# A column roll on one core: long row pieces spread over 13 DMA engines instead of 16

## The chip, the core and the metric

The kernel runs on one core of one Trainium2 chip. The metric is device time in microseconds (us) of one execution, and lower is better. A core has 16 DMA engines, which the profile counts together; SP and ACT issue transfers on one hardware queue each (q1 and q10 in the profile), and POOL (GpSimd) issues on a software queue (q0). TensorE does nothing in this kernel.

## What is computed

```python
x = np.random.randn(8192, 8192).astype(np.float32)   # 268.4 MB
shift = 100
return np.roll(x, shift, axis=1)
```

Every row of 8192 numbers (32 KB) is moved 100 places to the right, and its last 100 numbers come to its front. Nothing is calculated; 268.4 MB are read from HBM and 268.4 MB are written.

## The kernel before, in words

The kernel cuts each output row in two. With `s = 100`, the cut is at `a = 256` (line 20 rounds 100 up to 128, line 22 adds 128), and `g = a - s = 156`.

**Long pieces** are columns 256 to 8191 of the output: 7936 numbers, 31,744 bytes for each row. They go from HBM to HBM without a stop in SBUF. The rows are cut into 128 blocks of 64. A block is viewed as `e=16` groups of `j=4` neighbouring rows, and one `dma_start` on line 43 takes row `j` of all 16 groups: 16 rows of 31,744 bytes, whose starts are 4 rows apart. Rows with even `j` are issued by SP and rows with odd `j` by ACT. In the last four blocks each piece is cut into two halves of 15,872 bytes at `mid`. Per queue that makes 248 transfers of full pieces and 16 of halves. The framework lets each queue have four of its transfers under way: the issue of one waits until the fourth before it has landed (the first wait of each queue stands behind four issues).

**Heads** are columns 0 to 255 of the output, 8.4 MB in all. They go through SBUF, in 16 steps `k` of 512 rows. Per step POOL issues three reads: `t` (line 72), for three of every four rows one contiguous run of 256 numbers that holds the end of the row before and the start of the row itself; and two short reads into `h` (lines 73 and 76) for the rest. DVE copies both parts of `t` to their places in `h` (lines 74 and 77). All `t` and `h` tiles have buffers of their own, so nothing waits for a buffer. After the last read POOL issues 16 writes of `h` to the output (line 80), each as 512 rows of 1 KB. All head transfers have 128 partitions, or 512 rows, as their outer dimension.

Nothing else orders the three queues among each other. There is no other work.

Of the kernel before, what the change touches and what calls it, by code (L numbers as in the profile page):

```python
# [1 line left out]

# [4 lines left out]


@with_exitstack
def kernel(  # L10
    ctx: ExitStack,
    tc: tile.TileContext,
    x: bass.AP,
    shift: int,
    out: bass.AP,
):
    nc = tc.nc
    n_rows, n_cols = x.shape
    s = shift % n_cols
    a = -(-s // 128) * 128  # L20
    if 0 < a <= 384 and a + 128 <= n_cols:
        a += 128
    g = a - s
    P = nc.NUM_PARTITIONS
    engines = [nc.sync, nc.scalar]
    n_chunks = 16
    rows = n_rows // n_chunks

    xm = x.rearrange("(c e j) w -> c j e w", e=16, j=4)
    om = out.rearrange("(c e j) w -> c j e w", e=16, j=4)
    if a < n_cols:
        blocks = n_rows // 64
        mid = (a + n_cols) // 256 * 128
        for c in range(blocks):
            parts = ((a, mid), (mid, n_cols)) if c >= blocks - 4 and a < mid else ((a, n_cols),)  # L40
            for j in range(4):
                for lo, hi in parts:
                    engines[j % 2].dma_start(out=om[c, j, :, lo:hi], in_=xm[c, j, :, lo - s:hi - s])
    if a == 0:
        return


    if a > 512:
        for i in range(n_chunks):
            r = slice(i * rows, (i + 1) * rows)  # L50
            nc.gpsimd.dma_start(out=out[r, :s], in_=x[r, n_cols - s:])
            if g > 0:
                nc.gpsimd.dma_start(out=out[r, s:a], in_=x[r, :g])
        return

    Q = 4  # L60
    n_st = n_rows // (P * Q)
    reads = ctx.enter_context(tc.tile_pool(name="reads", bufs=n_st))
    heads = ctx.enter_context(tc.tile_pool(name="heads", bufs=n_st))
    xt = x.rearrange("(k p q) c -> k p q c", q=Q, p=P)
    ot = out.rearrange("(k p q) c -> k p q c", q=Q, p=P)
    tiles = []
    for k in range(n_st):
        t = reads.tile([P, Q - 1, a], x.dtype)
        h = heads.tile([P, Q, a], x.dtype)
        lead = bass.AP(tensor=x.tensor, offset=(k * P * Q + 1) * n_cols - s,  # L70
                       ap=[[Q * n_cols, P], [n_cols, Q - 1], [1, a]])
        nc.gpsimd.dma_start(out=t[:], in_=lead)  # L72
        nc.gpsimd.dma_start(out=h[:, Q - 1, :s], in_=xt[k, :, Q - 1, n_cols - s:])  # L73
        nc.vector.tensor_copy(h[:, :Q - 1, :s], t[:, :, :s])  # L74
        if g > 0:
            nc.gpsimd.dma_start(out=h[:, 0, s:], in_=xt[k, :, 0, :g])  # L76
            nc.vector.tensor_copy(h[:, 1:, s:], t[:, :, s:])  # L77
        tiles.append(h)
    for k, h in enumerate(tiles):
        nc.gpsimd.dma_start(out=ot[k, :, :, :a], in_=h[:])  # L80


# [1 line left out]
_INS = ['x', 'shift']  # L84
_OUTS = [((8192, 8192), 'float32')]

_NUMBERS = {'shift': 100}


# [26 lines left out]
```

## Time and profile before

| what | value |
|---|---|
| time, median of 3 runs | 816.8 us (815.75 to 818.27) |
| span of the profiled execution, first to last instruction | 828.0 us |
| DVE busy / POOL busy | 12.3 us / 41.3 us |
| bytes moved by DMA | 276.90 MB, mean 334 GB/s |
| HBM read + written | 268.44 MB + 268.44 MB, 648 GB/s over the span |

The median is of runs that were not profiled. For the profiled execution the page gives the span alone: its transfers begin 2.1 us after the span's start and the last of them ends 1.3 us before the span's end, so the span is taken as its own time. It is 11.2 us (1.4%) above the median.

A transfer from HBM to HBM counts once in the GB/s of the DMA lines, and twice (read and written) in HBM traffic. A "packet" of the long pieces is one row: 31,744 bytes carried by one DMA engine. After each there is a packet of 4 bytes that counts the transfer's completion, so half of the packets of q1 and q10 are these. The share in the queue lines is the time of the packets as a share of 16 engines' time.

### The profile page before, as it was taken

Reading aid. Unit: us, or ns where it says so; the run is one execution under the profiler, and the core shown is the slowest. Engines: PE = TensorE matmul, PEld = TensorE weight load, DVE = VectorE, ACT = ScalarE, POOL = GpSimd, SP = SyncE. Lnnn points to the kernel's source line nnn. Section 1 sums busy time; section 2 is a strip of 40 time slices with the busy share of each in tenths; the row PEclk is TensorE's granted clock in tenths of the full one; section 3 lists DMA queues with packets and bytes.
Section 4 is the critical chain, followed back from the end, with each engine's and each line's share of the span. In section 5 each row is a group of like instructions: output and inputs, shape, how many; then the busy total and the mean of one; then the engine's idle time right before and its main releaser. Section 6 shows DMA issues by size and latency. Waiting matters only on the chain. (4 is left out here: it accounts for less than half of the span.)

```text
span 828.0 us, 689 instructions
## 1 busy us (share of the span) xinstructions
DVE 12.3 (1%) x32; POOL 41.3 (5%) x68
## 2 busy tenths in 40 slices
DVE  0000000000010000000000000000000000000000
POOL 2011000000021100000000000000000000000000
DMA  9999999999999999999999999999999999999998
GB/s 308 340 350 334 344 340 337 337 339 344 337 342 348 352 351 345 354 339 346 347 341 344 333 325 325 319 330 333 330 324 322 335 330 328 322 331 328 327 314 300
DMA packets 22278, 276.90 MB, mean 334 GB/s; under 512 B 9473, under 2 KB 9729, under 8 KB 13825
## 3 DMA queue, kind: packets, MB, share of 16 engines
q1 hardware_dynamic: 8448, 130.04, 46.1%
q10 hardware_dynamic: 8448, 130.04, 44.7%
q0 software_dynamic: 5376, 16.78, 8.4%
q14 instruction: 6, 0.04, 0.0%
HBM read 268.44 MB, written 268.44 MB: 648 GB/s over the span
## 5 line engine op out<-in xcount | busy, mean ns | idle before, releaser
L80 POOL DMA_DIRECT2D out_dram<-h x16 | 11.5, 724 | 126.6 <-DMA out_dram<-h 86.8
L76 POOL DMA_DIRECT2D h<-in_x_dram x16 | 8.7, 542 | 141.4 <-DMA t<-in_x_dram 141.4
L72 POOL DMA_DIRECT2D t<-in_x_dram x16 | 12.2, 762 | 30.8 <-DMA h<-in_x_dram 30.0
L73 POOL DMA_DIRECT2D h<-in_x_dram x16 | 8.9, 559 | 39.9 <-DMA h<-in_x_dram 39.9
L74 DVE COPY h<-t 128x300 f32<-128x300 f32 x16 | 6.1, 382 | 260.2 <-DMA t<-in_x_dram 260.2
L77 DVE COPY h<-t 128x468 f32<-128x468 f32 x16 | 7.5, 467 | 0.0
L97 POOL MEMSET const-float32-0.0<- 128x1 f32 x1 | 0.1, 99 | 0.2 <-issue 0.2
L97 POOL MEMSET const-bfloat16-1.0<- 128x1 bf16 x1 | 0.1, 102 | 0.0
L97 POOL MEMSET const-float32-1.0<- 128x1 f32 x1 | 0.1, 99 | 0.0
L97 POOL MEMSET const-uint8-127<- 128x1 uint8 x1 | 0.1, 99 | 0.0
## 6 DMA issues: line engine op xcount, KB each, us to landing
out_dram<-in_x_dram ACTq DMA_DIRECT2D x248, 496.0 KB, 12.7
out_dram<-in_x_dram SPq DMA_DIRECT2D x248, 496.0 KB, 12.7
out_dram<-h POOLq DMA_DIRECT2D x16, 512.0 KB, 108.2
t<-in_x_dram POOLq DMA_DIRECT2D x16, 384.0 KB, 50.6
out_dram<-in_x_dram SPq DMA_DIRECT2D x16, 248.0 KB, 6.0
out_dram<-in_x_dram ACTq DMA_DIRECT2D x16, 248.0 KB, 5.9
h<-in_x_dram POOLq DMA_DIRECT2D x16, 78.0 KB, 43.2
h<-in_x_dram POOLq DMA_DIRECT2D x16, 50.0 KB, 49.9
```

The lines of the kernel that those rows point to most:

```text
L72: nc.gpsimd.dma_start(out=t[:], in_=lead)
L73: nc.gpsimd.dma_start(out=h[:, Q - 1, :s], in_=xt[k, :, Q - 1, n_cols - s:])
L74: nc.vector.tensor_copy(h[:, :Q - 1, :s], t[:, :, :s])
L76: nc.gpsimd.dma_start(out=h[:, 0, s:], in_=xt[k, :, 0, :g])
L77: nc.vector.tensor_copy(h[:, 1:, s:], t[:, :, s:])
L80: nc.gpsimd.dma_start(out=ot[k, :, :, :a], in_=h[:])
L97: nc = _bacc.Bacc("TRN2", target_bir_lowering=False, num_devices=1)
```

## The change

The long pieces of the first rows are issued in blocks of 52 rows, viewed as `e=13` groups of `j=4` rows. One transfer then has 13 rows of 31,744 bytes instead of 16. `K * 4` is 52; the rest of 8192 rows after whole blocks of 52 is 28, and the loop adds 52 until the tail is a multiple of 16 and at least 256, which is 288. So the code takes 152 blocks of 52 rows, 7904 rows in all, and then 288 rows as before with `e=16`: one block of 64 with whole pieces, and the last 224 rows in halves. (A short description that came with the change speaks of 7696 and 496 rows; the code gives 7904 and 288.) Per queue that is 304 transfers of 13 whole rows, 2 of 16 whole rows and 14 of 16 halves. The heads, with POOL's and DVE's instructions and their order, are the same.

```diff
+    K = 13
+    tail = n_rows % (K * 4)
+    while tail % 16 or tail < 256:
+        tail += K * 4
 
+    def copies(r0, e, js, halves):
+        xm = x[r0:r0 + e * js, :].rearrange("(e j) w -> j e w", j=js)
+        om = out[r0:r0 + e * js, :].rearrange("(e j) w -> j e w", j=js)
+        mid = (a + n_cols) // 256 * 128
+        parts = ((a, mid), (mid, n_cols)) if halves and a < mid else ((a, n_cols),)
+        for j in range(js):
+            for lo, hi in parts:
+                if lo < hi:
+                    engines[j % 2].dma_start(out=om[j, :, lo:hi], in_=xm[j, :, lo - s:hi - s])
 
-    xm = x.rearrange("(c e j) w -> c j e w", e=16, j=4)
-    om = out.rearrange("(c e j) w -> c j e w", e=16, j=4)
-    if a < n_cols:
-        blocks = n_rows // 64
-        mid = (a + n_cols) // 256 * 128
-        for c in range(blocks):
-            parts = ((a, mid), (mid, n_cols)) if c >= blocks - 4 and a < mid else ((a, n_cols),)
-            for j in range(4):
-                for lo, hi in parts:
-                    engines[j % 2].dma_start(out=om[c, j, :, lo:hi], in_=xm[c, j, :, lo - s:hi - s])
+    r0 = 0
+    while r0 + tail < n_rows:
+        copies(r0, K, 4, False)
+        r0 += K * 4
+    while r0 < n_rows:
+        js = min(4, (n_rows - r0) // 16)
+        copies(r0, 16, js, r0 + 256 >= n_rows)
+        r0 += 16 * js
```

## The prediction

> **What bounds the kernel now.** I read the page first, then the queue lines of single stretches of the span, then the waits of the issuing queue.
>
> ```profile
> span 828.0 us, 689 instructions
> DMA  9999999999999999999999999999999999999998
> ...
> q1 hardware_dynamic: 8448, 130.04, 46.1%
> q10 hardware_dynamic: 8448, 130.04, 44.7%
> q0 software_dynamic: 5376, 16.78, 8.4%
> ...
> HBM read 268.44 MB, written 268.44 MB: 648 GB/s over the span
> ```
>
> All 16 DMA engines are busy from end to end: 46.1 + 44.7 + 8.4 = 99.2%. No compute engine matters (DVE 12.3 us). But "busy" has two meanings here: an engine that moves at its own pace, or one whose packet is stretched by something shared. Three stretches tell them apart: heads being read, heads being written, long pieces alone.
>
> ```profile
> q10 hardware_dynamic: 2277, 36.03, 41.8%
> q1 hardware_dynamic: 2303, 36.35, 40.3%
> q0 software_dynamic: 2738, 7.55, 17.6%
> ```
>
> This is 5 to 240 us. Long pieces hold 82.1% of 16 engines, 13.1 engines' worth. Their packets took 0.821 x 16 x 235 = 3087 us, and 72.38 MB / 31,744 B = 2280 of them make 1.354 us each. HBM traffic is (2 x 72.38 + 7.55) / 235 us = 648 GB/s.
>
> ```profile
> q1 hardware_dynamic: 2325, 37.11, 46.3%
> q10 hardware_dynamic: 2309, 36.61, 42.8%
> q0 software_dynamic: 2611, 9.14, 11.7%
> ```
>
> 240 to 480 us: 14.3 engines' worth, by the same working 1.473 us a packet, 652 GB/s.
>
> ```profile
> q1 hardware_dynamic: 2892, 45.94, 50.8%
> q10 hardware_dynamic: 2893, 45.88, 48.5%
> ```
>
> 500 to 780 us, no heads: 15.9 engines' worth, 1.538 us a packet, 656 GB/s. From start to start it is 280 x 16 / 2892 = 1.549 us, so 0.011 us is lost between packets.
>
> ```profile
> q10 hardware_dynamic: 16, 0.51, 102.2%
> ```
>
> 3.5 to 4.7 us, the second packet of each engine: 1.022 x 16 x 1.2 / 16 = 1.226 us. The shortest long packet among the trace's records is 1.17 us (27.1 GB/s for one engine).
>
> So a packet that needs 1.17 to 1.23 us takes 1.35 with 13 engines on long pieces and 1.54 with 16, while the traffic stays at 648 to 656 GB/s. That is a shared limit near 656: more engines make each slower. Three engines fewer may therefore cost little. But the margin is small, and the sum below goes by one engine's load.
>
> ```profile
> SPq L43 <- DMA out_dram<-in_x_dram: 680.3, 260, 4.9
> ...
> L43 SPq DMA_DIRECT2D out_dram<-in_x_dram x264: 509/510/832, 0.7 to 820.3; - x132
> ```
>
> SP mostly waits for transfers to land (680.3 of 828 us), and an issue costs it 0.51 us.
>
> **The change part by part.**
>
> *Issuing.* Per queue 264 issues become 320 (304 + 2 + 14): 56 x 0.51 = 29 us more on SP and on ACT. The 680 us of waiting hide it; a transfer is issued every 828 / 320 = 2.6 us. Without that cover it would be 29 us. The window of four transfers a queue holds 13/16 of the bytes, but still 8 packets for each engine in use, so no engine on long pieces runs dry sooner. POOL and DVE do what they did, cost 0.
>
> *Load of one engine.* Before: 8192 / 16 = 512 rows and one sixteenth of the heads. After, an engine that is used: 7904 / 13 = 608 rows, 288 / 16 = 18 rows of the tail, and the same heads. The three others have heads and tail only, and are idle most of the time. Faster heads on these three end nothing sooner, since a head transfer lands when its last part does. So the end is set by the 13.
>
> *Heads.* 8.4% of 828 = 69.6 us an engine today. The reading stretch cost 0.176 x 16 x 235 = 662 us for 7.55 MB, the writing one 0.117 x 16 x 240 = 449 us for 9.14 MB; if reads became as cheap as writes, 16.78 MB x 49 us / 16 = 51 us. I take 70 for no relief, 51 for the range.
>
> *A long packet while heads are under way.* The 13 engines spend about a sixth of this stage on heads, so some 11 are on long pieces at a time, less than the 13.1 of the first stretch. Bounds: 1.17 (shortest) and 1.354 (that stretch). I take 1.23, the row of the second packets, and 1.24 with the gap.
>
> *A long packet with no heads.* Below, the ceiling: 13 x 31,744 B x 2 / 656 GB/s = 1.258 us. Above, 1.354 of the first stretch, where as many engines were on long pieces and head traffic came on top. The uncrowded pace would ask for 13 x 27.1 x 2 = 705 GB/s, more than any long stretch carried, so some crowding must stay. The first stretch, with all 16 engines at work, reached 648; fewer requesters should not come closer to the ceiling. I take the middle, 1.306, and 1.316 with the gap.
>
> *Sum.* The last head write was issued at 379.6 us and took some 108 us, so heads end near 488; packets ahead of theirs shrink by about a tenth, so 440. In that stage (440 - 70) / 1.24 = 298 long packets. The other 310 take 310 x 1.316 = 408 us. Tail 18 x 1.55 = 28 us, start and end 3.4 us (as now). 440 + 408 + 28 + 3.4 = 879 us of span. The median stood at 816.8 / 828.05 = 0.9864 of the span: 867 us. Ends of this case: 1.18 with heads and the ceiling's 1.268 after give 844.6, so 833 us; 1.364 in both stages gives 931, so 918 us.
>
> The Trainium skill speaks on both sides. "DMA: Bandwidth & Descriptors", Rules for kernel authors, tells an author to use all 16 engines and to choose the outer dimension for that, which speaks against 13; taken alone, as if engines were the limit, it makes the long rows 608/512 as dear. The same page's Specifications put one engine at about 27 GiB/s, 29 GB/s; by that a packet could take 1.10 us, an estimate, and 13 engines would carry 377 GB/s, more than the 328 of the last stretch, so nothing would be lost. The trace's best packet, 27.1 GB/s, is below that figure, and its crowded ones are at 20.6, so neither is used in the sum.
>
> **The rivals.**
>
> *Crowding goes with the three engines (faster).* All packets fall to 1.17 us and 0.011 of gap: 608 x 1.181 + 70 + 31.4 = 819 span, 808 us; with heads at 51, 800 and 789 us. It decides below a slot of (828 - 31.4 - 70) / 608 = 1.195 us, or 1.226 with the cheap heads. For it: the second packets at 1.226 and the many records at 1.17 even in the last stretch. Against: it needs some 670 GB/s on average where no stretch passed 656. A limit that falls with the number of streams could do this; 648, 652 and 656 at 13.1, 14.3 and 15.9 engines' worth don't show one.
>
> *Packets don't get shorter (much slower).* If the 1.538 us belongs to each engine and its neighbours, not to a total: 608 x 1.549 + 70 + 31.4 = 1043, 1029 us. Against: the 1.354 of the first stretch.
>
> *The 13 rows don't stay on 13 engines.* If successive transfers start on other engines, all 16 share the rows as before. Then the rate is that of now, about 817 us. No row of this trace names an engine. The Trainium skill ("DMA: Bandwidth & Descriptors", on why a DMA increments its semaphore by 16) says that hardware queues use the lowest-numbered k engines, k being the largest divisor up to 16, here 13; no run so far shows it.
>
> **How the numbers follow.** A difference of 0.3%, 2.5 us, is about what the runs can tell from none. The forecast has 0.76 (833 to 918, all slower), the much slower case 0.06, rotation 0.06 (no change), the gain 0.12. The range leaves out the slowest case, the last few us of the forecast, and about half of the gain: 808 to 914, with 867 as the likeliest. Faster 0.12, same 0.06, slower 0.82.
>
> **What the profile after would show.** Right: DMA share near 13.3 of 16 engines (tenths of 8 and 9), about 315 GB/s in the stretches without heads, some 1.3 us from start to start over 13 engines, and full sharing only in the last 30 us; heads done before 488 us. The forecast is wrong if the share stays at 99% (rotation), if the last stretches carry over 335 GB/s (crowding gone), or if they carry under 290 (packets not shorter). Of the steps, the packet with no heads is the weakest: 0.05 us on it moves the end by 15 us.

## The result and the profile after

| | median | runs |
|---|---|---|
| before | 817.95 us | 6 (815.75 to 819.06) |
| changed | 823.01 us | 6 (820.65 to 826.37) |

The changed kernel takes 1.0067 times as long, 95% interval 1.005 to 1.0083: slower, as forecast, but by 5 us and not by 50.

Page of the changed kernel (the DMA row in tenths of 16 engines, then the queues with packets, MB and share):

```profile
span 821.5 us, 801 instructions
DMA  7888888888888888888888788888888888888898
...
q1 hardware_dynamic: 8416, 130.04, 39.3%
q10 hardware_dynamic: 8416, 130.04, 38.0%
q0 software_dynamic: 5376, 16.78, 6.1%
...
HBM read 268.44 MB, written 268.44 MB: 653 GB/s over the span
```

The engines are now busy for 83% instead of 99% (39.3 + 38.0 + 6.1 = 83.4%, 13.3 of 16 engines, as the prediction had it), and the bytes arrive in almost the same time. That fits rows that stay on 13 engines, since 13/16 is 81%; run 4 settles it. Heads hold 6.1% where they held 8.4%.

Queue lines of the changed kernel, 5 to 240 us, then 500 to 780 us:

```profile
q1 hardware_dynamic: 2271, 36.26, 37.0%
q10 hardware_dynamic: 2273, 35.91, 36.0%
q0 software_dynamic: 3267, 9.14, 12.8%
```

```profile
q1 hardware_dynamic: 2909, 46.19, 41.4%
q10 hardware_dynamic: 2916, 46.38, 40.1%
```

With the prediction's working: while heads are read a long packet takes 0.730 x 16 x 235 / 2273 = 1.21 us (1.354 before), and without heads 0.815 x 16 x 280 / 2916 = 1.25 us (1.538 before). Without heads the HBM traffic is 2 x 92.57 MB / 280 us = 661 GB/s; as one-way bytes that is 331 GB/s, between the 315 that the prediction expected and the 335 above which it called itself wrong.

Waits of SP's queue, and its issues (duration in ns, minimum, median, maximum):

```profile
SPq L43 <- DMA out_dram<-in_x_dram: 567.1, 316, 3.8
...
L43 SPq DMA_DIRECT2D out_dram<-in_x_dram x320: 509/764/982, 0.7 to 814.1; - x160
```

An issue of 13 rows costs 0.76 us where one of 16 rows cost 0.51. With 56 more issues SP spends some 110 us more on issuing (320 x 0.764 against 264 x 0.51, an estimate from the medians), not 29, and its waits shrink by as much, from 680.3 to 567.1 us. It still waits for 567 us, so this is covered.

### The profile page after: what moved, and what is told of

Same layout as the page of the kernel before. It is cut to its first block, busy times and chain, and to the rows that moved or that the text cites. A ratio compares the mean times of both kernels' runs of the same rounds, so it can differ in the third digit from the quotient of the medians.

```text
span 821.5 us, 801 instructions
## 1 busy us (share of the span) xinstructions
DVE 12.0 (1%) x32; POOL 41.2 (5%) x68
## 3 DMA queue, kind: packets, MB, share of 16 engines
q1 hardware_dynamic: 8416, 130.04, 39.3%
q0 software_dynamic: 5376, 16.78, 6.1%
```

## The experiments

Times below are compared only within one set of runs on one chip. The kernel before itself took 826.4, 826.7 and 816.4 us in the three sets, and 818.0 beside the result.

**1. The kernel before, profiled again** (no edit).

> The kernel before, profiled once more, because its first profiled execution (span 828.0 us) stands 1.2% above its own median while the changed kernel's profiled span (821.5 us) is close to its median of 823.0. Expected: a span of about 816 us, long packets without heads at 1.52 us instead of 1.538, HBM traffic there of about 661 GB/s, as with 13 engines. If the span is 828 again, profiling itself costs this kernel 1.4% and the changed kernel nothing.

Median 826.67 us, its profiled span 824.0, and without heads 1.53 us a packet and 658 GB/s. The level of this set is 1% above that of the result; the expectation of 816 us missed. The profiled execution was one of the timed ones: 825.8 us of time for 824.0 of span, so what lies around the span is some 2 us. Profiling has no cost of 1.4%. So the 828.0 us and the 816.8 us from which the prediction took its ratio of 0.9864 are probably of two levels of speed; the time of that first profiled execution is not on record.

**2 to 4. Other numbers of engines.** In each, `K = 13` becomes `K = 14` (below), `12` or `8`, and the tail follows by its own rule.

```diff
-    K = 13
+    K = 14
```

> K = 14 instead of 13: 7840 rows on 14 engines, 352 on 16. Theory S (one shared limit of about 661 GB/s of HBM traffic, packets stretch until they fit into it, an engine alone needs 1.18 us): packets without heads 14 x 63.5 KB / 661 GB/s = 1.345 us, same traffic, time between those of 16 and 13 engines, 816 to 823 us. Rival F (fewer streams use HBM better, so 13 gains in the stretches and loses elsewhere): traffic without heads below that of 13 engines, by 1% or more.

> K = 12: 7920 rows on 12 engines, 272 on 16. Theory S: 12 engines at their own pace ask for 12 x 63.5 KB / 1.19 us = 640 GB/s, below the limit, so the engines are the bound all through: packets 1.18 us, 660 x 1.19 + 26 + 50 + 3 = 865 us of span, 5% slower than 13. Rival F: crowding stays even below the limit, packets stay at 1.22 us or more, 890 us or more.

> K = 8: 7936 rows on 8 engines, 256 on 16. It measures a packet that nothing crowds. Theory S: nearly every packet at 1.174 to 1.18 us, 992 x 1.19 + 25 + 45 + 3 = 1253 us, traffic without heads 8 x 63.5 / 1.19 = 427 GB/s. Rival F, or neighbours on the same engines' ports that hinder each other: a mean above 1.2 us, over 1270 us. If the rows did not stay on 8 engines, the time would be near 820 us.

| engines | time | ratio to before (95%) | long packet without heads | HBM traffic there |
|---|---|---|---|---|
| 16 (run 1) | 826.67 us | 1.0004 (0.9989 to 1.0019) | 1.53 us | 658 GB/s |
| 14 | 831.71 us | 1.006 (1.004 to 1.0079) | 1.35 us | 658 GB/s |
| 12 | 862.89 us | 1.044 (1.0419 to 1.0461) | 1.20 us | 637 GB/s |
| 8 | 1252.21 us | 1.5152 (1.5109 to 1.5196) | 1.20 us | 427 GB/s |

The last two columns come from the queue lines of 500 to 780 us. Those with 16 engines, 14, 12 and 8:

```profile
q1 hardware_dynamic: 2912, 46.23, 51.5%
q10 hardware_dynamic: 2900, 45.84, 47.7%
```

```profile
q10 hardware_dynamic: 2905, 46.23, 44.6%
q1 hardware_dynamic: 2903, 45.94, 42.6%
```

```profile
q1 hardware_dynamic: 2808, 44.57, 38.0%
q10 hardware_dynamic: 2811, 44.67, 37.3%
```

```profile
q1 hardware_dynamic: 1878, 29.81, 25.3%
q10 hardware_dynamic: 1883, 29.97, 25.0%
```

With 8 engines the share is 50.3%, half of the 16, and the time is 1252 us, not near 820: the rows of a transfer stay on as many engines as it has rows. In these stretches the engines in use have next to no gaps: 99.2, 87.2, 75.3 and 50.3% are busy of 100, 87.5, 75 and 50%. So it is not the window of four transfers a queue that limits the traffic. A packet that nothing crowds takes 0.503 x 16 x 280 / 1883 = 1.20 us, with its 4-byte companion in it, and with 12 engines it is the same. So below 13 the engines' own pace decides (theory S gave 865 and 1253 us of span; 861.5 and 1250.7 were measured). With 14 and 16 engines the traffic is the same 658 GB/s and the packet gives way. That is a shared limit. Twelve engines at their own pace stay below it with 637 GB/s, and 13 at 1.20 us a packet would ask for 688, so it is reached between 12 and 13 engines. What failed is the expected time of 14 engines, 816 to 823 us on a chip that takes 826 for 16: against its partner it loses 0.6%, about as much as 13.

The profiles of runs 1 and 2 also show where the 14 engines lose. From 5 to 240 us their HBM traffic is (2 x 71.81 + 8.22) / 235 = 646 GB/s against (2 x 72.55 + 8.02) / 235 = 652 with 16, and from 240 to 480 us it is 649 against 657, by the same working. Without heads both have 658. The loss is in the stage with heads.

**5 and 6. Without heads**, on 16 and on 13 engines. The kernel returns before line 60 of the kernel before, and at the same place (line 69) in the changed one.

```diff
+    return
     Q = 4
     n_st = n_rows // (P * Q)
```

> The kernel before without the heads: columns 0 to 255 of the output are not written, POOL and DVE do nothing. Long pieces on 16 engines all through. With the shared limit of 661 GB/s: 2 x 260.05 MB / 661 = 787 us and about 6 for the ends: 793 us. It is the partner of the next run.

> The changed kernel without the heads (columns 0 to 255 not written). Theory H (the changed kernel loses its 5 us where heads and long pieces share the 13 engines, whose time is then full): without heads 13 engines cost the same as 16 within 0.3%, 608 x 1.256 + 28 + 3.4 = 795 us. Theory D (the loss lies in the last 288 rows and their end, or in 13 streams reaching the limit a little less): still 4 to 6 us slower than its partner.

799.24 and 801.11 us, ratios to the kernel before of 0.9666 (0.9648 to 0.9683) and 0.9688 (0.967 to 0.9706). Both are 6 us above what was expected, in a set where the kernel before takes 826.7 us and not 818. The intervals overlap; the medians differ by 1.9 us or 0.23%, and the profiled spans are 797.8 and 797.7. Without heads 13 engines do nearly as well as 16. That speaks for theory H over D, though it does not exclude a loss of 1 to 2 us that has nothing to do with heads.

**7 and 8. One kind of block first, the other after**, with the change of blocks after 4992 rows, past the last head. Run 7 has this ahead of the loop of 52-row blocks:

```diff
+    for _ in range(78):
+        copies(r0, 16, 4, False)
+        r0 += 64
```

Run 8 cuts that loop short, and the rest goes on 16 engines:

```diff
-    while r0 + tail < n_rows:
+    for _ in range(96):
         copies(r0, K, 4, False)
         r0 += K * 4
```

> The first 4992 rows (78 blocks of 64, about 500 us, past the last head) on 16 engines, the next 2912 in blocks of 52 on 13, the last 288 on 16. Theory H: the head stage is that of the kernel before, so the loss is gone: 817 to 818 us, same as before. Theory D: the end is that of the changed kernel, so most of the 5 us stay: 821 to 823.

> The first 4992 rows (96 blocks of 52, past the last head) on 13 engines, the other 3200 on 16. Theory H: the head stage is that of the changed kernel, 822 to 823 us. Theory D: the end is that of the kernel before, 817 to 819 us.

16 first and 13 after: 826.88 us, 1.0005 (0.9992 to 1.0018), no difference. 13 first and 16 after: 830.13 us, 1.0044 (1.003 to 1.0057). The intervals are apart. The times in us that were expected miss by the level of this set; the ratios came out as theory H had them. The loss goes with the 13 engines of the first 4992 rows, which take some 510 us, not with those after them or with the end. HBM traffic says the same: from 5 to 240 and from 240 to 480 us it is 652 and 659 GB/s with 16 engines (run 7), 649 and 654 with 13 (run 8); from 600 to 780 us, where they have changed places, it is 657 with 13 and 656 with 16. Sixteen engines first and 13 after is the best use of 13 found here, and it gains nothing.

**9 and 10. Both kernels, profiled on one chip** (no edits).

> The kernel before, profiled on the chip of the next three, so that its stages stand beside theirs. Two chips gave 826.4 and 826.7 us for it and one 818.0. Expected: HBM traffic of 650 to 660 GB/s with heads, 656 to 661 without.

> The changed kernel on the same chip. Theory H (the loss lies in the stage with heads, where 13 engines are full at their own pace of 1.20 us a packet): traffic in the first 480 us 0.5 to 1% below its partner's, equal within 0.3% from 480 to 780 us; time 4 to 6 us longer. Rival D (the loss is in the end or in a lower limit for 13 streams): equal with heads, lower after 480 us or in the last 40 us.

816.22 us, and 820.71 us with a ratio of 1.0053 (1.0034 to 1.0073): 4.5 us. Queue lines of 5 to 240 us, 240 to 480 and 500 to 780, first of the kernel before:

```profile
q1 hardware_dynamic: 2328, 37.11, 43.3%
q10 hardware_dynamic: 2339, 36.99, 41.0%
q0 software_dynamic: 2644, 7.25, 15.5%
...
q1 hardware_dynamic: 2367, 37.65, 45.9%
q10 hardware_dynamic: 2364, 37.53, 43.6%
q0 software_dynamic: 2672, 9.32, 10.9%
...
q1 hardware_dynamic: 2919, 46.29, 49.9%
q10 hardware_dynamic: 2921, 46.42, 49.4%
```

and of the changed kernel:

```profile
q1 hardware_dynamic: 2287, 36.51, 36.9%
q10 hardware_dynamic: 2290, 36.19, 36.3%
q0 software_dynamic: 3231, 9.03, 12.7%
...
q1 hardware_dynamic: 2356, 37.37, 37.8%
q10 hardware_dynamic: 2360, 37.56, 37.1%
q0 software_dynamic: 2139, 7.72, 8.3%
...
q1 hardware_dynamic: 2936, 46.61, 41.4%
q10 hardware_dynamic: 2940, 46.73, 40.0%
```

HBM traffic (long bytes twice, head bytes once) of before and changed: 661 and 657 GB/s in the first stretch, 665 and 657 in the second, 662 and 667 in the third. In bytes the changed kernel falls behind by 1.0 and 2.1 MB while there are heads, worth 4.7 us at 662 GB/s, and catches up by 1.2 MB, 1.8 us, in the third stretch. Theory H had the place and sign of the first part; the gain without heads, 0.6%, is one that neither theory had put down. This pair of profiles shows it; in runs 7 and 8 it is 0.2% (657 against 656 GB/s), too little to build on.

The first 5 us cost something too. The windows of before, then changed (duration, engines, clock, DMA share, GB/s):

```profile
0.00:5.00 5.00, 0.00 (x0) 3.92 (x10) 1.00 0.60 203
```

```profile
0.00:5.00 5.00, 0.00 (x0) 3.91 (x10) 1.00 0.53 170
```

33 GB/s less for 5 us is 0.17 MB of copies, twice that in HBM traffic, 0.5 us. The first long packet starts at 2.45 us in the changed kernel and at 2.12 in the kernel before. Together the three parts make 4.7 - 1.8 + 0.5 = 3.4 us, where the two profiled spans are 3.1 us apart (815.4 and 818.5).

**11 and 12. More head traffic**, in both kernels. A step's added read goes into a tile `u` that nobody uses.

```diff
+    extra = ctx.enter_context(tc.tile_pool(name="extra", bufs=n_st))
...
         nc.gpsimd.dma_start(out=t[:], in_=lead)
+        u = extra.tile([P, Q, a], x.dtype)
+        nc.gpsimd.dma_start(out=u[:], in_=xt[k, :, :, :a])
```

> The kernel before with one more read a step on POOL: columns 0 to 255 of the step's 512 rows into a tile that nobody uses, 8.39 MB in all, half as much head traffic again. Both theories: 8.39 MB / 656 GB/s = 13 us more than before, if the limit is the shared one.

> The changed kernel with the same additional read. Theory H: the stage in which the 13 engines are full gets longer by half, so the distance to its partner grows from 5 us to 7 to 10 us. Rival D: the distance stays at 5 us.

831.95 us, 1.0189 (1.0164 to 1.0213), and 835.78 us, 1.0238 (1.0214 to 1.0262). Against runs 9 and 10 the added read costs 15.7 and 15.1 us, more than the 13 expected. The distance is 3.8 us, not 7 to 10: theory H's size is refuted, and taken by itself this looks as D had it. HBM traffic in GB/s, by the same working as above:

| stretch | 16 engines (run 11) | 13 engines (run 12) |
|---|---|---|
| 5 to 240 us | 662 | 655 |
| 240 to 480 us | 655 | 658 |
| 480 to 660 us, mostly with heads | 665 | 660 |

With 16 engines the traffic drops to (2 x 72.70 + 11.68) / 240 = 655 GB/s in the second stretch, where run 9 had 665, but not in the other two. So 13 engines still bring less in two of the three stretches with heads, and over all of them the difference is 0.4% (660 and 657 GB/s), where it was 1.0% in the first 480 us of runs 9 and 10 (663 and 657). The loss did not grow with the head traffic. Why the second stretch turned round is open, and no run varied the amount of heads further.

## Why the prediction was right on the sign and wrong on the size

*Right.* The engines in use set the pace when there are few of them, a shared limit does when there are many, and 13 stands close to the border, so no gain came. The share of busy engines came out as stated. Two rivals fell: packets did get shorter (1.25 us, not 1.54), and the rows stayed on 13 engines (share 83%, half with 8). The gain that was to come if crowding went did not come either: packets fell to 1.21 us only where heads filled the rest of the 13 engines' time. SP's additional issues were hidden, although each cost half as much again as the sum had it.

*Luck, in the sign.* By the terms of the sum the traffic would have been (2 x 298 x 13 x 31,744 B + 16.78 MB) / 440 us = 597 GB/s with heads and 13 x 2 x 31,744 B / 1.316 us = 627 without. The changed kernel carried 653 and 659 in the two stretches with heads and 661 without. So nearly all of the loss that the forecast had put down, in both stages, was not there. "Slower" came true by what was left, about 1% of the traffic while heads are under way; without heads 13 engines carried no less than 16. The prediction had measured 648 to 656 and called it a shared limit, but never held its own sum against it.

*Wrong, in three terms of the sum and its conversion.*

- The packet with no heads was put at 1.306 us, between the ceiling's 1.258 and 1.354, on the argument that fewer requesters should not come closer to the ceiling. They come just as close: 661 GB/s, 1.25 us, and 13 x 280 / 2916 = 1.248 us from start to start instead of 1.316. That is 310 x 0.068 = 21 us of the 57 between the forecast's 879 us of span and the measured 821.5. The lower bound, not the middle, was the value; runs 2 and 3 place the border between 12 and 13. This is the largest of the failed steps, and the prediction itself called it the weakest.
- Heads were kept at 70 us an engine. 6.1% of 821.5 us is 50 us, at the lower bound of 51 again. That frees room for 16 more long packets in their stage, some 20 us at the end.
- The packet in the head stage took 1.21 us, 1.24 was used with its gap: by the same working some 7 packets, 9 us. Together the three make 50 of the 57 us.
- The step from span to time, 0.9864, took 12 us off, where runs 1 and 9 show that some 2 us are added. By luck it hid a quarter of the other three errors. The first profile's 828.0 us lies nearer to the slower level (824.0 in run 1) than to the 816.8 us beside it.

With these values the same sum gives (452 - 50) / 1.21 = 332 packets up to the end of the heads at 451 to 452 us (the last head write is issued at 356.0 and takes 95 to 96 us), 276 x 1.248 = 344 us after it, 28 for the tail and 3.4 for the ends: 828 us of span, 0.8% above the 821.5 measured.

The three terms had one mistake in common. The bounds on each held within 2%, but the value was taken between them or at today's, as if fewer engines on long pieces relieved each term only in part. All three fell to or towards their lower ends together, which is what one shared limit would do.

*Where the 5 us are.* Shown by runs 7 to 10, and by runs 1 and 2 for 14 engines: in the stage with heads, where 13 engines bring 0.5 to 1.3% less HBM traffic than 16. Why is not shown. Theory H argues that an engine there works at 1.21 us a packet, near its pace alone, with its time full, so it cannot make use of what the limit still allows. Against it as the whole cause: run 2, with 14 engines at 1.28 us or more a packet and thus not at their own pace, loses 0.8 to 1.1% of the traffic in that stage too, and run 12 did not lose more with more heads. The cause of these 5 us stays open.

The Trainium skill, "DMA: Bandwidth & Descriptors", Rules for kernel authors, says to use all 16 engines. The runs agree with its direction: 14, 13, 12 and 8 engines on the long pieces all lose. But the price is not the engines' share: three of 16 engines left out cost 0.5 to 0.7%, and the fourth, which takes the kernel below the shared limit, costs close to 4% more.

## What to carry to other kernels

A DMA engine that reads as busy may be waiting inside its packets; divide the queue's busy time by its packets in stretches of different load, and compare with the shortest packet. If traffic is constant and the packet's time is not, as here, the limit is shared, and engines can be left out at a small price until the sum of their own paces meets it. Then hold the forecast's own sum against that traffic: a stage that comes out well below it needs a reason. When several costs have one cause, put them at the same end of their bounds, and take the level of a chip from times measured beside each other.

## What was not expected of the hardware

- The limit of HBM traffic for this copy is 656 to 667 GB/s, and it does not depend visibly on whether 13, 14 or 16 engines ask for it.
- Issuing a transfer of 13 rows takes SP 0.76 us in the median and one of 16 rows 0.51; with `K = 12` the median is 0.74, with 14 it is 0.77, with 8 it is 0.63 (the last is the line below):

```profile
L43 SPq DMA_DIRECT2D out_dram<-in_x_dram x512: 509/627/794, 0.7 to 1244.1; - x171
```

- The same heads became cheaper as fewer engines carried long pieces. They took 50 us an engine in run 10 (6.1% of 818.5 us) and 63 in run 9 (7.7% of 815.4); in runs 1 to 4, with 16, 14, 12 and 8 engines, 71, 57, 47 and 46 us (8.6, 6.9, 5.4 and 3.7% of the spans).
- The limit does not stretch all packets alike. From 500 to 780 us the trace's records of long packets show 80% at the shortest time of 1.18 us or less and 4% at 1.6 us or more with 13 engines (run 10); with 16 (run 9) they show 24% and 35%. Their means, 1.24 and 1.52 us by the queue lines of those runs, are made of both kinds.
- The same kernel took 816.4, 818.0, 826.4 and 826.7 us in four sets of runs, 1.3% apart, more than the change that was to be measured.
